# A hybrid decoder layer on one core: output projection's weight tiles split once for two token groups, gate tiles kept in SBUF, fetches one ahead

## The chip, the core and the metric

The kernel runs on one core of a Trainium2 chip. The metric is the device time of one execution in microseconds; the time before is the median of three runs.

## What is computed

One layer of a decoder for 1024 prompt tokens and 8 sequences of 8 new tokens (1088 tokens, width 1024, float32). The reference, cut to what matters here:

```python
h = _rmsnorm(x, g_mix_in)
gate_a, x_a, q, k, v, z_c, xbc, dt_raw = _split_cols(h @ w_in)
...
out_a = h_a * jax.nn.gelu(gate_a)
...
mix = jnp.concatenate([out_a, out_b, out_c], axis=-1) @ w_out
x = x + _rmsnorm(mix, g_mix_out)

hf = _rmsnorm(x, g_ffn_in)
g_f, u_f = jnp.split(hf @ w_gate_up, 2, axis=-1)
x = x + _rmsnorm((jax.nn.silu(g_f) * u_f) @ w_down, g_ffn_out)
```

`out_a` is a gated linear recurrence, `out_b` dilated attention, `out_c` a state space mixer.

## The kernel before

Tokens lie along the free axis, in three groups of 364, 362 and 362 (`GROUPS`); features lie on partitions, in eight chunks of 128. Every product is exact to float32 by three passes: each operand is split into a rounded high part and the rest (`round`, a cast on ScalarE or VectorE; `rest`, a subtraction on VectorE), and TensorE multiplies high by high, low by high and high by low (`mm3`, `x3`). A weight tile of 128x1024 (512 KB) is fetched into one of two raw buffers (`raws`), and split into a pair (`pair`).

The order of the work is set on the host by a planner, the class `Flow`: tasks are Python generators that yield until a condition holds; each operation is costed and handed in with a rank (`RANKS`: "prep" before "mix" before "main"), and the planner writes one fixed instruction list for each engine. VectorE, ScalarE, GpSimd and SyncE (the DMA queue) take the ready operation of the best rank; TensorE's matmuls are emitted as their generators come to them. What a row of the profile calls L345 is the line of the planner that emits all operations but matmuls (L431) and transposes (L435).

The stages around the change:

- `setup` and `first_products`: six warming matmuls on zeros, x loaded and scaled, the first two weight tiles of the input projection multiplied as x arrives.
- The input projection takes weight tiles 0 to 22 in turn. Each tile and group ends in a PSUM bank that `spill` multiplies by the inverse norm on VectorE and, for most tiles, writes to DRAM (`pd`). The last two, `GATE_T` and the next, are the gate.
- `gate`: six pieces (two tiles j, three groups g). A piece is loaded from `pd` with the recurrence's state `hd` into one of three sets of buffers (`shared`), goes through gelu (a square and a tanh on ScalarE, four steps on VectorE), and is split into `XH` and `XL`, the split mixer outputs that the output projection reads. The three sets are free for this when the state space mixer is done (`c_done`).
- `first_out`: the output projection of group 0. Tile n is multiplied over seven of eight chunks while the attention still runs, and copied to SBUF; the eighth chunk comes behind attention's last unit, from one tile of its own (`LATE_T`).
- `second_half`: groups 1 and 2, `out_tile` for n from 0 to 7 each. The weight tiles come from a stream of items (`make_stream`, `streamed`), eight for group 1 and the same eight again for group 2; an item's fetch and split are handed in together (`plain`) as a pair comes free.
- `out_norm(g)`, of rank "prep": first inverse norm (`inverse_norm`: a sum over partitions by matmul, a power on GpSimd, a transpose, a broadcast by matmul), product and residual sum for eight chunks, second inverse norm, scaling into `Y`.
- `right_factors(i)`: for token half i (two quarters of 272 tokens) the factors of a Strassen-like scheme of seven products: parts of `Y` are split, subtracted and split again, each on 128x1088 elements. Factors 1 and 2 need group 0 and 1, 7 and 3 of the first half need group 2; 6, 4, 5 come by subtractions in place.
- `plain_gate_up`, then `gate_up` and `down` on these factors, with weight tiles from the same stream, to the end.

## Time and profile before

| | us |
|---|---|
| median of three runs (1339.01 to 1341.4) | 1340.19 |
| the profiled execution | 1338.55 |
| its span, first to last instruction | 1336.8 |
| mean granted TensorE clock (share of full) | 0.991 |

Times in the rows below are from the start of the span. PE is TensorE's matmuls, PEld its weight loads, DVE VectorE, ACT ScalarE, POOL GpSimd, SP SyncE, which issues the DMAs. A float32 matmul of the program (one of the few that are not split) makes several records. "Idle before" is the time that an engine had nothing to do ahead of a group, with what ended it. Names are the program's without their numbers: t is an SBUF tile, bank a PSUM bank.

### The profile page before, as it was taken

Reading aid. Unit: us, or ns where it says so; the run is one execution under the profiler, and the core shown is the slowest. Engines: PE = TensorE matmul, PEld = TensorE weight load, DVE = VectorE, ACT = ScalarE, POOL = GpSimd, SP = SyncE. Lnnn points to the kernel's source line nnn. Section 1 sums busy time; section 2 is a strip of 40 time slices with the busy share of each in tenths; the row PEclk is TensorE's granted clock in tenths of the full one; section 3 lists DMA queues with packets and bytes.
Section 4 is the critical chain, followed back from the end, with each engine's and each line's share of the span. In section 5 each row is a group of like instructions: output and inputs, shape, how many; then the busy total and the mean of one; then the engine's idle time right before and its main releaser. Section 6 shows DMA issues by size and latency. Waiting matters only on the chain.

```text
span 1336.8 us, 22870 instructions
## 1 busy us (share of the span) xinstructions
PE 1300.9 (97%) x8871; PEld 1243.3 (93%) x8871; DVE 933.1 (70%) x1878; ACT 585.3 (44%) x1095; POOL 19.9 (1%) x36
## 2 busy tenths in 40 slices
PE   9999999999998989989899999999999999999997
PEld 8999988999997878989899999999999999999786
DVE  7799884776858887888766666666567855555852
ACT  7355451752856675544322222222223444444422
POOL 0000000000000000000000000000000000000000
PEclk9999999999999899999999999999999999999999
DMA  6122466456547437635122113221222477865661
GB/s 212 29 68 72 133 184 207 137 175 189 160 130 231 141 103 236 193 116 182 40 97 97 48 51 97 97 80 44 72 97 97 158 237 221 293 210 183 204 205 48
DMA packets 95946, 186.33 MB, mean 139 GB/s; under 512 B 15346, under 2 KB 62686, under 8 KB 95838
## 3 DMA queue, kind: packets, MB, share of 16 engines
q1 hardware_dynamic: 95838, 184.88, 43.9%
q8 instruction: 69, 1.13, 0.3%
q14 instruction: 39, 0.32, 0.1%
HBM read 144.45 MB, written 40.40 MB: 138 GB/s over the span
## 4 chain that ended last, share of the span: by engine, by line
PE 86%; DMA 5%; DVE 3%; issue 2%; ACT 2%; SPq 1%; DVEq 0%; POOLq 0%; POOL 0%; ACTq 0%
PE bank L431 84%; DVE t L345 3%; PE bank L435 2%; DMA t<-pd 2%; ACT t L345 2%; DMA t<-in_w_out_t 2%; DMA t<-in_w_in_t 1%; SPq L345 1%; DMA t<-in_w_gu_t 1%; DMA t<-in_xT 0%; DVEq L2007 0%; POOLq L2007 0%; POOL t L345 0%; DVEq L345 0%; ACTq L345 0%
## 5 line engine op out<-in xcount | busy, mean ns | idle before, releaser
L431 PE MATMUL bank<-t,t 128*128 128x272 f32 (+8 forms) x8505 | 1274.5, 313 | 27.1 <-DVE t L345 13.8
L431 PEld LDWEIGHTS bank<-t,t 128*128 128x128 f32 (+2 forms) x8505 | 1205.0, 187 | 78.6 <-DVE t L345 23.0
L345 DVE TENSOR_TENSOR t<-t,t 128x512 fp32r<-128x512 f32 (+13 forms) x633 | 458.8, 749 | 128.7 <-ACT t L345 112.5
L345 ACT CAST t<-t 128x512 fp32r<-128x512 f32 (+6 forms) x346 | 251.2, 748 | 404.7 <-PE bank L431 159.2
L345 DVE TENSOR_TENSOR t<-t,bank 128x272 f32<-128x272 f32 (+4 forms) x283 | 126.9, 453 | 123.8 <-PE bank L431 122.4
L345 DVE TENSOR_TENSOR t<-bank,t 128x362 f32<-128x362 f32 (+11 forms) x227 | 112.1, 511 | 73.3 <-ACT t L345 43.4
L345 ACT ACTIVATE t<-t,t 128x128 f32<-128x128 f32 (+17 forms) x212 | 132.8, 666 | 34.1 <-DVE t L345 14.7
L345 ACT ACTIVATE t<-t 128x272 f32<-128x272 f32 (+10 forms) x173 | 91.1, 537 | 95.0 <-DVE t L345 90.8
L345 ACT COPY t<-bank 128x272 f32<-128x272 f32 (+8 forms) x122 | 44.5, 372 | 101.3 <-PE bank L431 89.0
L345 DVE TENSOR_TENSOR t<-t 128x272 f32<-128x272 f32 (+8 forms) x147 | 67.5, 459 | 2.8 <-ACT t L345 0.2
L345 DVE SCALAR_TENSOR_TENSOR t<-t,t,t 128x1112 f32<-128x1112 f32 (+7 forms) x68 | 56.6, 860 | 4.7 <-ACT t L345 4.0
L435 PE MATMUL bank<-t,t 128*128 128x128 f32 (+5 forms) x354 | 54.7, 276 | 1.5 <-ACT t L345 0.8
L345 ACT ACTIVATE t<-bank 128x272 f32<-128x272 f32 (+7 forms) x55 | 23.3, 428 | 65.2 <-PE bank L431 63.1
L345 DVE CAST t<-t 128x512 fp32r<-128x512 f32 (+6 forms) x68 | 30.4, 449 | 26.7 <-PE bank L431 13.5
L345 ACT CAST t<-bank 128x512 fp32r<-128x512 f32 (+2 forms) x72 | 35.0, 514 | 31.4 <-PE bank L435 30.5
L435 PEld LDWEIGHTS bank<-t,t 128*128 128x128 f32 (+5 forms) x354 | 40.7, 139 | 7.4 <-DVE t L345 2.4
L345 DVE CUSTOM_DVE_ANT_0 t<-bank,t 128x512 f32<-128x512 f32 (+3 forms) x75 | 39.9, 548 | 7.3 <-PE bank L431 6.7
L345 POOL TENSOR_TENSOR t<-t,t 128x3 f32<-128x3 f32 (+1 forms) x17 | 17.0, 1000 | 1148.2 <-DVE t L345 1082.9
L345 DVE SCALAR_TENSOR_TENSOR t<-t,t,bank 128x362 f32<-128x362 f32 (+4 forms) x55 | 28.2, 550 | 1.6 <-PE bank L431 1.4
L345 DVE SCALAR_TENSOR_TENSOR t<-t 128x54 f32<-128x54 f32 (+5 forms) x39 | 17.9, 458 | 2.5 <-DMA t<-yd 1.6
L345 ACT ACTIVATE t<-bank,t 128x362 f32<-128x362 f32 (+1 forms) x29 | 15.7, 560 | 8.9 <-PE bank L431 8.8
L345 DVE SCALAR_TENSOR_TENSOR t<-t,t 128x1024 f32<-128x1024 f32 (+2 forms) x20 | 17.5, 889 | 1.5 <-ACT t L345 1.4
(20 smaller groups left out, 72.6 us busy)
## 6 DMA issues: line engine op xcount, KB each, us to landing
t<-in_w_dn SPq DMA_DIRECT2D x66, 512.0 KB, 3.7
t<-in_w_gu_t SPq DMA_DIRECT2D x52, 512.0 KB, 4.6
t<-in_w_out_t SPq DMA_DIRECT2D x24, 512.0 KB, 4.2
hidd<-t SPq DMA_DIRECT2D x44, 272.0 KB, 2.1
t<-in_w_in_t SPq DMA_DIRECT2D x21, 512.0 KB, 4.9
t<-hidd SPq DMA_DIRECT2D x44, 176.0 KB, 3.8
t<-pd SPq DMA_DIRECT2D x24, 256.0 KB, 4.1
pd<-t SPq DMA_DIRECT2D x28, 181.0 KB, 3.2
```

Source lines behind the costliest of these rows:

```text
L345: self.flow.note(self.name, what, args, kw, lambda: getattr(self.engine, what)(*args, **kw))
L431: self.flow.product(out, [w, x], start, d, lambda: self.nc.tensor.matmul(out, w, x, **how))
L435: self.flow.product(out, [x], True, d, lambda: self.nc.tensor.transpose(out, x, ident))
```

## The change

- Seven splits of weight tiles instead of sixteen in the second half of the output projection: in `second_half`, tile 7 is used from the pair in which `first_out` left it, and tiles 0 to 6 are split once and serve groups 1 and 2. Their places are a spare pair, five pairs of factor buffers (`IN_TURN`, lent until the factors are formed) and the pair of the late chunk. Group 2 takes them in the order 7, 0, 6, 1 to 5. The first half's factors 7 and 3 now wait until all of group 2's tiles are read (`out_read`).
- `fetch` is split from `plain`: the next item's tile is fetched one ahead, into the other raw buffer.
- The gate's tiles are evicted from PSUM straight into SBUF (`gate_at`) instead of to DRAM and back, and three tasks, one for each group, start as soon as their group's eviction is handed in. Tiles of the gate wait for `c_done` before that; `first_out` waits for all six pieces.
- A rank "norm" between "prep" and "mix" for `out_norm` and the first factors; the factors' subtractions and later splits go to "mix", behind the beginning of the second step of the plain gate-up (`plain_begun`).
- Residual sums are called through another name of the same VectorE queue; eight warming matmuls instead of six, and four more among the first products; the planner costs a matmul anew; outputs of the plain gate-up lie in two new buffers, which become raw buffers when it is done.

In all TensorE has 8254 instructions instead of 8253, VectorE 1760 instead of 1743, ScalarE 863 instead of 896 and SyncE 531 instead of 551.

```diff
-WARM = 6
+WARM = 4
...
+FIRST, IN_TURN = 5, (7, 3, 6, 4, 5)
...
-    RANKS = {"prep": 0, "mix": 1, "main": 2}
+    RANKS = {"prep": 0, "norm": 1, "mix": 2, "main": 3}
...
-            d = max(math.prod(out.shape[1:]), 120) * (1 if x.dtype == F32R else 4) / 2400 + 0.0025
+            n = math.prod(out.shape[1:])
+            d = max(n / 2400 + 0.0135, 0.109) if x.dtype == F32R else max(n, 128) / 600 + 0.0025
...
+            if i >= GATE_T:
+                nc.vector.tensor_mul(self.gate_at(i - GATE_T, g), b, self.rs[:, sl])
+                return
...
+                        if i >= GATE_T:
+                            yield lambda: self.c_done
...
-            nc.vector.memset(squares[0][:, 0:256], 0.0)
-            for _ in range(WARM):
-                self.mm(self.bank[7][:, 0:128], squares[0][:, 0:128], squares[0][:, 128:256], start=True, stop=True)
+            self.zeros = self.alloc(256)
+            nc.vector.memset(self.zeros, 0.0)
+            self.warm(2 * WARM)
...
+                    if k == i == g == 0:
+                        self.warm(WARM)
...
-        F.spawn(self.gate(), group="b")
+        temps = Rot([self.mg[:, 6 + n] for n in range(3)])
+        for g in range(3):
+            F.spawn(self.gate(g, temps), group="b")
...
-        self.splits = [self.pair()] + self.splits
+        self.spare = self.pair()
+        self.open("first")
+        parts = {FIRST: self.factor()}
+        self.open("halves0")
+        parts.update({p: self.factor() for p in IN_TURN[:-1]})
+        self.lent = [[x.rearrange("p k t -> p (k t)")[:, :1024] for x in parts[p]] for p in IN_TURN]
         self.mixers_done = True
         yield lambda: 0 in self.x1_done and not F.pending([self.mg_words])
         self.release(self.mg_pool)
-        self.open("first")
-        first = self.alloc(4, QT, dt=F32R), self.alloc(4, QT, dt=F32R)
-        self.open("halves0")
-        self.XT = [self.half_parts(0, first)]
+        self.open("rest")
+        parts.update({p: self.factor() for p in PRODUCTS if p not in parts})
+        F.spawn(self.right_factors(0, parts), cls="prep")
+        self.XT = [parts]
...
-    def gate(self):
+    def gate_at(self, j, g):
+        return self.mg[:, 3 * j + g, :GROUPS[g][1]]
+
+    def gate(self, g, temps):
         nc, F = self.nc, self.flow
+        c0, w = GROUPS[g]
+        sl = slice(c0, c0 + w)
         for j in range(2):
-            yield lambda: self.emitted > GATE_T + j and self.c_done
-            for g, (c0, w) in enumerate(GROUPS):
-                sl = slice(c0, c0 + w)
-                x, p, h = [t[:, :w] for t in self.shared()]
-                nc.sync.dma_start(x, self.pd[GATE_T + j][:, sl])
-                nc.sync.dma_start(h, self.hd[j][:, sl])
-                nc.scalar.activation(p, x, AF.Square)
-                nc.vector.tensor_scalar(p, p, 0.044715, 1.0, op0=ALU.mult, op1=ALU.add)
-                nc.vector.tensor_mul(p, p, x)
-                nc.scalar.activation(p, p, AF.Tanh, scale=math.sqrt(2.0 / math.pi))
-                nc.vector.scalar_tensor_tensor(x, p, 1.0, x, op0=ALU.add, op1=ALU.mult)
-                nc.vector.scalar_tensor_tensor(h, x, 0.5, h, op0=ALU.mult, op1=ALU.mult)
-                yield lambda: self.free_at[g] == W_OUT_T
-                self.round(self.XH[:, j, sl], h)
-                self.rest(self.XL[:, j, sl], h, self.XH[:, j, sl])
-                self.in_done.add((j, g))
+            yield lambda: self.free_at[g] > GATE_T + j
+            x, p, h = self.gate_at(j, g), temps()[:, :w], self.ev()[:, :w]
+            nc.sync.dma_start(h, self.hd[j][:, sl])
+            nc.scalar.activation(p, x, AF.Square)
+            nc.vector.tensor_scalar(p, p, 0.044715, 1.0, op0=ALU.mult, op1=ALU.add)
+            nc.vector.tensor_mul(p, p, x)
+            nc.scalar.activation(p, p, AF.Tanh, scale=math.sqrt(2.0 / math.pi))
+            nc.vector.scalar_tensor_tensor(x, p, 1.0, x, op0=ALU.add, op1=ALU.mult)
+            nc.vector.scalar_tensor_tensor(x, x, 0.5, h, op0=ALU.mult, op1=ALU.mult)
+        for j in range(2):
+            x = self.gate_at(j, g)
+            self.round(self.XH[:, j, sl], x)
+            self.rest(self.XL[:, j, sl], x, self.XH[:, j, sl])
+            self.in_done.add((j, g))
...
-            self.flow.spawn(self.out_norm(g), cls="prep")
+            self.flow.spawn(self.out_norm(g), cls="norm")
...
+            yield lambda: all((j, g) in self.in_done for j in range(2) for g in range(3))
...
-                self.streamed(0, len(self.splits) - 1)
+                self.streamed(0)
...
-        for _ in range(2):
-            self.items += [lambda pair, t=W_OUT_T + n: self.plain(pair, t) for n in range(KT)]
+        self.items += [lambda pair, t=W_OUT_T + n: self.plain(pair, t) for n in range(KT - 1)]
...
-        self.slots, self.sent, self.hids = {}, 0, {}
-
-    def streamed(self, i, held=0):
-
-        last = min(i + len(self.splits) - 1 - held, len(self.items) - 1)
+        self.slots, self.sent, self.hids, self.places = {}, 0, {}, {}
+        order = [LATE_T] + [W_OUT_T + n for n in range(KT - 1)]
+        order += [W_GU_T + which * NF + f for f in range(PLAIN) for which in range(2)]
+        self.tiles_of = dict(enumerate(order))
+        self.tiles_of.update({self.dn_base + n: W_DN_T + n % NF for n in range(1, 3 * NF)})
+        self.fetched = []
+
+    def streamed(self, i, held=0, alone=False):
+
+        ahead = 0 if i < self.plain_base or alone else len(self.splits) - 1 - held
+        last = min(i + ahead, len(self.items) - 1)
         for j in range(self.sent, last + 1):
             with self.prio("prep"):
-                pair = self.splits.pop(0)
-                self.splits.append(pair)
+                if j in self.places:
+                    pair = self.places[j]
+                else:
+                    pair = self.splits.pop(0)
+                    self.splits.append(pair)
                 self.items[j](pair)
+                if self.tiles_of.get(j + 1) is not None and not self.fetched:
+                    self.fetch(self.tiles_of[j + 1])
             self.slots[j] = pair
         self.sent = max(self.sent, last + 1)
         return self.slots[i]
...
+        self.nc.sync.dma_start(raw.rearrange("p (n c) -> p n c", c=128) if t == LATE_T else raw, src)
+        self.fetched.append((t, raw))
+
+    def plain(self, pair, t):
+        if not self.fetched:
+            self.fetch(t)
+        u, raw = self.fetched.pop(0)
+        assert u == t
+        hi, lo = [x[:, :raw.shape[-1]] for x in pair]
         self.round(hi, raw)
         self.rest(lo, raw, hi)
...
-        i = 1
-        for g in (1, 2):
-            for n in range(KT):
-                yield from self.out_tile(g, n, self.streamed(i))
-                i += 1
+        last, late = self.splits
+        self.splits = [last, self.spare, late]
+        slots = [self.spare] + self.lent + [late]
+        self.places = dict(enumerate(slots, 1))
+        held = [(KT - 1, last)] + list(enumerate(slots))
+        for at, (n, pair) in enumerate(held):
+            self.streamed(min(at + 2, KT - 1))
+            yield from self.out_tile(1, n, pair, at)
+        for at, (n, pair) in enumerate(held[:2] + held[-1:] + held[2:-1]):
+            yield from self.out_tile(2, n, pair, at)
+            self.out_read = at + 1
+            if at < len(self.splits):
+                self.streamed(KT + at, alone=True)
...
-        self.XT.append(self.half_parts(1))
-        self.raws.items += [self.alloc(1024) for _ in range(2)]
-        self.raws.i = 1
+        self.XT.append({p: self.factor() for p in PRODUCTS})
+        F.spawn(self.right_factors(1, self.XT[1]), cls="prep")
+        self.late_raws = [self.alloc(1024) for _ in range(2)]
...
-        def split(p, x):
+        first = "mix" if i else "norm"
+
+        def split(p, x, cls="mix"):
             hi, lo = parts[p]
-            self.round(hi, x)
-            self.rest(lo, x, hi)
-
-        split(1, b11)
-        split(2, b21)
+            with self.prio(cls):
+                self.round(hi, x)
+                self.rest(lo, x, hi)
+
+        def sub(out, x, y):
+            with self.prio("mix"):
+                nc.vector.tensor_sub(out, x, y)
+
+        split(1, b11, first)
+        split(2, b21, first)
         self.quarters = max(self.quarters, 1)
-        yield lambda: i + 1 in self.x1_done
+        yield lambda: i + 1 in self.x1_done and (i or self.out_read == KT)
         if i == 0:
-            split(7, b12)
-        split(3, b22)
+            split(7, b12, first)
+        split(3, b22, first)
         self.quarters = 2
-        self.nc.vector.tensor_sub(b11, b12, b11)
-        self.nc.vector.tensor_sub(b12, b22, b12)
-        self.nc.vector.tensor_sub(b22, b22, b11)
+        yield lambda: i or self.plain_begun
+        sub(b11, b12, b11)
+        sub(b12, b22, b12)
+        sub(b22, b22, b11)
         split(6, b22)
-        self.nc.vector.tensor_sub(b21, b21, b22)
+        sub(b21, b21, b22)
         split(4, b21)
         split(5, b11)
...
+            out = outs()
...
+                self.plain_begun = f > 0
...
         self.plain_done = True
+        self.raws = Rot(self.raws.items + self.late_raws)
+        self.raws.i = 1
```

The order in which instructions stand, at two places. The first is VectorE around the last evictions of the input projection (t2 is `XL`, t17 the eviction buffers, t110 before and t111 after the buffers of the gate, bank0 and bank6 the projection's banks). Before, the second gate tile's group 0: its last two gelu steps and its rest (the last row), which stands 64 VectorE instructions behind its eviction:

```order
L345 TENSOR_TENSOR t2_74<-t110_2152,t1_73 128x362
L345 TENSOR_TENSOR t136_2181<-bank7_69,t136_2181 64x256
L345 ISA t122_2167,t141_2186<-bank1_63,t146_2191 128x128
L345 ISA t141_2186 128x1
L345 SCALAR_TENSOR_TENSOR t110_2152<-t110_2152 128x364
L345 TENSOR_SCALAR t110_2152<-t110_2152 128x362
L345 SCALAR_TENSOR_TENSOR t110_2152<-t110_2152 128x364
L345 TENSOR_TENSOR t110_2152<-t110_2152 128x362
L345 TENSOR_SCALAR t110_2152<-t110_2152 128x362
L345 TENSOR_TENSOR t2_74<-t110_2152,t1_73 128x364
```

Now the same piece: the step ahead of these rows is its first one, and the rest is again the last row, 20 instructions behind its eviction:

```order
L347 TENSOR_TENSOR t2_74<-t111_2132,t1_73 128x364
L347 TENSOR_TENSOR t111_2132<-bank6_68,t16_99 128x362
L347 TENSOR_TENSOR t111_2132<-t111_2132 128x364
L347 TENSOR_TENSOR t2_74<-t17_100,t1_73 128x364 x3
L347 SCALAR_TENSOR_TENSOR t111_2132<-t111_2132 128x364
L347 TENSOR_TENSOR t134_2158<-bank3_65,t133_2157 128x512
L347 SCALAR_TENSOR_TENSOR t111_2132<-t111_2132,t17_100 128x364
L347 TENSOR_TENSOR t136_2160<-bank4_66,t135_2159 128x384
L347 TENSOR_TENSOR t111_2132<-bank0_62,t16_99 128x362
L347 ISA t127_2151,t145_2169<-bank2_64,t147_2171 128x512
L347 ISA t145_2169 128x1
L347 TENSOR_TENSOR t2_74<-t111_2132,t1_73 128x364
```

The piece's whole chain now stands between the evictions of the second tile's other groups (the two rows that read bank6 and bank0 and t16); before it stood behind all of them, and behind attention's rows.

The second place is VectorE at the third group's norm, ahead of the first half's factors (t156 before and t157 after are `Y` and the groups' sums; outputs of 128x1088 with an fp32r source pair are rests of factors; t7 is the spread norm). Before, rests and subtractions in place stand ahead of the third group's first residual product (last row):

```order
L345 TENSOR_TENSOR t172_5240<-t156_4872,t171_5239 128x1088
L345 TENSOR_TENSOR t156_4872<-t156_4872 128x4x272
L345 TENSOR_TENSOR t168_5236<-t156_4872,t167_5235 128x1088
L345 TENSOR_TENSOR t156_4872<-t156_4872 128x4x272
L345 TENSOR_TENSOR t7_82<-bank3_65,t3_78 6x256
L345 TENSOR_TENSOR t156_4872<-t156_4872 128x4x272
L345 TENSOR_TENSOR t162_5230<-t156_4872,t161_5229 128x1088
L345 TENSOR_SCALAR t7_82<-bank3_65,t3_78 6x106
L345 TENSOR_TENSOR t158_4874<-t188_5539,t157_4873 128x1024
L345 TENSOR_TENSOR t170_5238<-t156_4872,t169_5237 128x1088
L345 TENSOR_TENSOR t156_4872<-t156_4872,bank6_68 128x272
L345 TENSOR_TENSOR t156_4872<-t156_4872,bank3_65 128x362
```

Now the second group's scaling, then two rests, then the third group's norm and its first residual product and sum:

```order
L347 SCALAR_TENSOR_TENSOR t157_4851<-t157_4851,t4_79,bank1_63 128x362 x8
L347 TENSOR_TENSOR t16_99<-t16_99,t17_100 128x362
L347 TENSOR_TENSOR t163_4863<-t157_4851,t162_4862 128x1088
L347 TENSOR_TENSOR t165_4865<-t157_4851,t164_4864 128x1088
L347 TENSOR_SCALAR t8_83<-bank3_65 128x3
L347 CAST t8_83<-t8_83 128x3
L347 TENSOR_TENSOR t8_83<-t8_83 128x3
L347 TENSOR_TENSOR t7_82<-bank3_65,t3_78 6x256
L347 TENSOR_SCALAR t7_82<-bank3_65,t3_78 6x106
L347 TENSOR_TENSOR t157_4851<-t157_4851,bank3_65 128x362
L347 TENSOR_TENSOR t188_5527<-t188_5527,bank6_68 128x272
L347 TENSOR_TENSOR t157_4851<-t157_4851,t17_100 128x362
```

The subtractions and three of the rests have moved behind the third group's residual.

## Rows read from the trace of the kernel before

**Rows 1.** The page, busy time by engine: us, share of the span, instructions.

```profile
PE 1300.9 (97%) x8871; PEld 1243.3 (93%) x8871; DVE 933.1 (70%) x1878; ACT 585.3 (44%) x1095; POOL 19.9 (1%) x36
```
**Rows 2.** Stretches (from:to, length): busy by engine, then PEclk, DMA share, GB/s.

```profile
421.60:437.10 15.50, 8.58 (x58) 6.55 (x57) 13.74 (x40) 13.32 (x32) 0.00 (x0) 0.97 0.64 190
437.10:501.60 64.50, 59.05 (x376) 54.37 (x377) 52.58 (x118) 44.60 (x96) 0.00 (x0) 0.93 0.40 121
501.60:511.40 9.80, 7.82 (x35) 6.58 (x36) 6.84 (x16) 3.32 (x6) 0.85 (x1) 0.83 0.70 224
511.40:564.00 52.60, 52.58 (x320) 51.23 (x320) 44.19 (x80) 29.49 (x49) 2.05 (x2) 1.00 0.68 211
564.00:590.00 26.00, 21.50 (x134) 19.79 (x133) 20.62 (x35) 10.27 (x15) 2.62 (x2) 0.93 0.49 162
590.00:645.00 55.00, 50.80 (x383) 49.71 (x382) 49.90 (x77) 28.07 (x41) 1.87 (x1) 0.97 0.40 129
645.00:1336.80 691.80, 683.99 (x4812) 665.50 (x4811) 426.94 (x764) 229.09 (x409) 4.27 (x5) 1.00 0.40 129
```
**Rows 3.** Timeline of PE, 420 to 646 us: start, length, group, [idle before, releaser].

```profile
437.14 9.11 PE L431 MATMUL bank<-t,t 128*128 128x364 f32 x36 [2.27 <-ACT t L345]
...
507.79 0.85 PE L431 MATMUL bank<-t,t 128*128 128x362 f32 x2 [1.50 <-ACT t L345]
...
583.72 0.39 PE L431 MATMUL bank<-t,t 128*128 128x272 f32 x1 [1.61 <-ACT t L345]
...
585.79 14.41 PE L431 MATMUL bank<-t,t 128*128 128x272 f32 x96 [1.68 <-DVE t L345]
...
638.45 0.39 PE L431 MATMUL bank<-t,t 128*128 128x272 f32 x1 [2.11 <-ACT t L345]
...
640.93 5.30 PE L431 MATMUL bank<-t,t 128*128 128x272 f32 x28 [2.09 <-DVE t L345]
```
**Rows 4.** Stretches in which the granted clock was 0.50, columns as in rows 2.

```profile
436.27:443.10 6.83, 5.96 (x19) 5.68 (x20) 5.19 (x10) 3.72 (x11) 0.00 (x0) 0.50 0.51 160
494.30:497.71 3.41, 3.41 (x15) 3.07 (x14) 3.28 (x7) 2.77 (x6) 0.00 (x0) 0.50 0.00 0
...
sum 20.47, PE 19.11 PEld 17.86 DVE 18.61 ACT 9.88 POOL 0.00; mean PE 3.82 PEld 3.57 DVE 3.72 ACT 1.98 POOL 0.00
```
**Rows 5.** Timeline of SP (DMA issues), 421 to 434 us.

```profile
431.42 1.17 SPq L345 DMA_DIRECT2D t<-pd  x2
```
**Rows 6.** Three stretches with VectorE nearly full, columns as in rows 2.

```profile
371.00:487.00 116.00, 107.56 (x732) 99.61 (x730) 85.93 (x223) 74.47 (x161) 0.00 (x0) 0.97 0.57 167
...
584.00:600.00 16.00, 14.32 (x97) 13.73 (x97) 16.00 (x20) 8.46 (x10) 0.00 (x0) 0.89 0.08 20
...
620.00:641.00 21.00, 16.80 (x129) 16.20 (x129) 20.27 (x26) 12.67 (x17) 0.00 (x0) 1.00 0.20 65
```
**Rows 7.** Instructions by line and shape, VectorE and ScalarE: busy us, mean ns, idle before.

```profile
L345 DVE TENSOR_TENSOR t<-t,t 128x1024 fp32r<-128x1024 f32 x125 | 152.6, 1223 | 78.6 <-ACT t L345 77.7
...
L345 DVE TENSOR_TENSOR t<-t,t 128x1088 fp32r<-128x1088 f32 x17 | 21.6, 1282 | 1.2 <-ACT t L345 1.2
...
L345 ACT CAST t<-t 128x1024 fp32r<-128x1024 f32 x111 | 116.3, 1048 | 148.8 <-DMA t<-in_w_dn 81.0 <-PE bank L431 19.1 <-DMA t<-in_w_in_t 17.5
```
**Rows 8.** The page's DMA issues: count, KB each, median us to landing.

```profile
t<-in_w_out_t SPq DMA_DIRECT2D x24, 512.0 KB, 4.2
```
**Rows 9.** Timeline of VectorE, 569 to 600 us.

```profile
570.47 0.16 DVE L345 TENSOR_SCALAR t<-bank 128x3 f32<-128x3 f32 x1 [0.48 <-PE bank L431]
...
572.71 0.77 DVE L345 CAST t<-t 128x1024 fp32r<-128x1024 f32 x2 [0.49 <-DMA t<-in_w_gu_t]
...
580.37 0.58 DVE L345 SCALAR_TENSOR_TENSOR t<-t,t,bank 128x362 f32<-128x362 f32 x1
```
**Rows 10.** Timeline of PE, 0 to 14 us.

```profile
1.22 2.93 PE L431 MATMUL bank<-t 128*128 128x128 f32 x12 [1.22 <-DVE t L345]
...
7.22 7.03 PE L431 MATMUL bank<-t,t 128*128 128x362 f32 x24 [1.23 <-ACT t L345]
```

60 lines of the change are left out of this document (30 added, 30 removed).

## The prediction

> **What bounds the kernel now.** I read the page first, for the shares [rows 1]. TensorE is busy for 1300.9 of 1336.8 us and its weight loads for 1243.3, so nothing that other engines gain is worth anything unless TensorE waits for it. All that a change of order can win is TensorE's 35.9 us without work, and what its clock loses after them. The next view is the table of stretches [rows 2]: from 645 us to the end (gate-up products and down projection, 691.8 us) TensorE has work for 683.99 us at full clock, so the change has little to win there. The idle time lies in four short places between 421 and 645 us. The third view, TensorE's timeline, names each wait and who ends it [rows 3]: ScalarE or VectorE each time, never another matmul. The fourth is the granted clock [rows 4]: five stretches at 0.50 (1.2 of 2.4 GHz) stand behind such waits (the group shows the longest, one of the other four, which are 3.41 us each, and the sum), with 19.11 us of TensorE work in them, which at full clock would have taken 9.6 us less. A wait therefore costs its length and about 1.7 us (half of 3.41) behind it, 3.0 us behind the longest.
>
> So the stock from which the change can draw, stretch by stretch (idle from rows 2, clock as half of the busy time in rows 4), is:
> - A, 421.6 to 437.1 (gate): 6.9 idle and 3.0 clock, 9.9 us
> - B, 437.1 to 501.6 (end of attention): 5.5 and 1.7, 7.2 us
> - C, 501.6 to 511.4 (second group's first tiles): 2.0 and 1.5, 3.5 us
> - D, 564 to 590 (norms, factors 7 and 3): 4.5 and 1.7, 6.2 us
> - E, 590 to 645 (first product): 4.2 and 1.7, 5.9 us
>
> Together 32.7 us.
>
> **The gate (A and B).** Before, a gate tile's group goes to DRAM and comes back: SyncE issues the loads for the second gate tile only at 431.42 us [rows 5], when one of three sets of temporaries has come free. Behind that stand a square and a tanh on ScalarE, four steps on VectorE and the split, and TensorE waits until 437.14 [rows 3]. The change takes out six writes and six reads, and lets each group's chain start at its own eviction. The order shows the whole chain of the second tile's first group standing within the evictions, so its rest is due 20 VectorE rows behind its eviction instead of 64. First products of the output projection now also wait for all six gate pieces, and the attention units run on meanwhile. Nothing is added on VectorE: an eviction, four steps and a rest for each piece, as before.
>
> But this is a stretch in which VectorE is nearly full: 13.74 of 15.5 us there [rows 2], 85.93 of 116.00 from 371 to 487 us [rows 6]. What no longer makes TensorE wait there is done elsewhere in the same 130 us, and seven weight splits of the second half are pulled up to its end as well. From both sides: nothing (the waits only move within A and B), or all 17.1 us. A's waits, the one at 437.14 with the clock behind it (2.3 and 3.0) above all, belong to the gate's chain and should go but for a rest of one; B's belong to attention's own chains of maxima and sums, which the change leaves as they are. So I take most of A and nothing of B: **−9.0**.
>
> **Second half of the output projection (C).** Before, sixteen tiles of 512 KB are fetched and split, eight for each group; now the last tile of the first group is used again and seven are split once. Gone are nine fetches (4.2 us from issue to landing each [rows 8], beside other work), nine casts (ScalarE 1.05) and nine rests (VectorE 1.22 [rows 7]): 9.4 us and 11.0 us of engines that are not the bound there; at 511.4 to 564 TensorE is busy 52.58 of 52.60 us [rows 2]. So the nine splits by themselves are worth **0**, hidden under the group's 192 matmuls; if that cover were gone they would cost 20. What pays is their time. The second group's first tile waits for nothing now: its pair is the one just used, and the next was fetched ahead. Before, TensorE waited 1.50 us at 507.79 for a pair whose raw tile had just landed, and ran at half clock behind that. From nothing to all 3.5; I take **−3.0**, since the norm of the first group still ends there.
>
> **Norms and factors (D).** Before, VectorE forms the second group's sums at 570.47 and reaches the scaling only at 580.37 [rows 9], 9.9 us for a chain of eight short steps, because weight splits stand between, one of them waiting for its tile. Factors 7 and 3 need this, and TensorE waits 1.61 and 1.68 us for them at 583.72 and 585.79 [rows 3]. In the change no split stands there, and the norms have a rank ahead of the splits and of the factors' subtractions. VectorE's next rows are the two rests of 1.28 us [rows 7] instead of five with four subtractions between. The gap between the two waits closes, and so does the clock's loss. The lower end is nothing (VectorE is full from 584 to 600, 16.00 of 16.00 us [rows 6]: what is put first displaces something), the upper 6.2. I take **−4.5**, as the norm's own chain (a power on GpSimd, a transpose, a broadcast) stays.
>
> **First product (E).** The waits at 638.45 and 640.93 (2.11 and 2.09) are for factor 6 of the second half of the tokens, behind VectorE's 20.27 busy of 21.00 us [rows 3, 6]. The third group's residual started late, since nine operations of 1088 elements stood ahead of it; with the order changed it starts some 11 us earlier (those nine by 1.28). TensorE's place for factor 6 is the same. So a wait of 4.2 us should be covered, against a new load of at most nine operations that come in between. From nothing to 5.9; I take **−4.4**. Late there next is that factor's own subtraction, which needs the third group's x1.
>
> **The start.** TensorE's six warming products end at 4.15 us; its second run of products comes in at 7.22 after a wait of 1.23, and takes 7.03 us for 24 matmuls [rows 10], 0.293 each against 0.164 later. Two warming products more ahead of it and four in between can bring the clock up earlier, worth 3.1 us if nothing else held the matmuls; but x arrives and is scaled no sooner. At the other end the six took 2.93, so two more cost 0.98 and four 1.95, of which the wait covers 1.23: +1.7. Between these I take **−0.5**, near nothing, since the wait shows the operands behind.
>
> **Edits at nothing.** "Residual sums on VectorE" swaps one name for the planner's for the same engine: no instruction changes engine. The planner's new matmul cost has no instruction of its own; it is in the order that I read. The plain gate-up's outputs in raw buffers that come later: gate-up streams 0.5 MB tiles under TensorE's 684 us.
>
> **Sum**: −9.0 −3.0 −4.5 −4.4 −0.5 = −21.4. The profiled execution took 1338.55 us, so 1317.15; the median of the runs is 1340.19, 1.64 above that execution, so **1318.8**.
>
> **Rivals.**
> 1. VectorE sets the pace of A and B, and the waits move. For it: its 13.74 of 15.5 us; its work up to the first group's norm rises by some 7 us of splits. Against it: 30 us of 116 are idle there. Then only C, D, E and the start come: −12.4, 1327.8. Chance 0.17.
> 2. VectorE's queue holds back what is behind it. The row at 570.47 and the 9.9 us after it [rows 9] show a scaling of half a microsecond waiting behind splits that themselves wait for a transfer. Seven splits now stand in one bunch in front of the first group's norm; should a fetch be late there, norms and factors all shift, and D and E keep their waits: −12.5, 1327.7. Against: the second and third group's products, over 60 us of TensorE, lie between. Chance 0.14. The Trainium skill has the rule, in "TensorE: Matmul & The Clock Gate", section "Architectural detail": ScalarE and VectorE take their instructions strictly in order, and only TensorE pulls weight loads ahead. By that rule the bunch holds the norm for as long as its slowest fetch; the trace agrees at 570.47, and shows no instruction of VectorE passing another.
> 3. All of it goes: 32.7 and the start's 0.5, 1307.0. For: every wait named has a cause that the change touches or moves. Against: attention's chains in B are as they were. Chance 0.10.
> 4. Slower: one tile ahead is too little. The seven tiles, if they go one by one, take 4.2 to land, 1.05 to be cast and 1.22 for the rest, 6.5 us each, against 24 matmuls of 0.164 (52.58 by 320 [rows 2]), 3.9 us. Seven times 2.5 is 17.7, and each wait leaves 1.7 at half clock, 11.9 in all; with only A, B's 9.0 and the start's 0.5 left as gains that is +20.1, 1360.3. It decides against the change from 5.3 us a tile on (21.4 by 7 is 3.1, of which 1.7 clock). Against: two raw buffers in turn make it 3.2 us a tile, and the planner issues the fetches while the first group still runs. Chance 0.08.
> 5. The order's gain is nil, since waits come up elsewhere by as much: 1340. Chance 0.05.
>
> **How the numbers follow.** A difference under 0.2% (2.7 us) cannot be told from none. The forecast has 0.46, with a range of its own from 1312 to 1326 (A and B between −4 and −14). Faster: 0.46 + 0.17 + 0.14 + 0.10 = 0.87; same 0.05; slower 0.08. The range leaves out rivals 4 and 5 and half of rival 3: 1309 to 1331, the upper end rivals 1 and 2 with 3 us for their unknowns.
>
> **What would show it.** A and B: no wait over 1 us for XH or XL between 420 and 440, and the granted clock at 1.00 there; if VectorE's busy share to the first norm is over 90% with TensorE waiting for it, it is rival 1. C: the second group's first tile follows the first group's last without a wait for a weight; waits of 2 us or more at a constant distance of some 6 us would be rival 4. D: the second group's scaling within 5 us of its sums. E: no wait of 2 us within the first product. The prediction is wrong if TensorE's busy time leaves 1300 by over 10 us (then the loss was clock, or matmuls), or if the stretch behind 645 us changes by over 5 us.

## The result and the profile after

The changed kernel takes 1325.51 us (median of four runs, 1324.68 to 1328.14), the kernel before 1340.03 beside it: a ratio of 0.9899, 95% interval 0.9881 to 0.9917, or 14.5 us less by the medians. It is 1% faster and lies inside the ranges of the prediction, at the upper edge of the narrower one (1312 to 1326). The forecast of 1318.8 was too low by 6.7 us: two thirds of the 21.4 us came. Rivals 1 and 2, at 1327.8 and 1327.7, are nearer in number; the stretches below show that what they describe is not what happened.

The page of the kernel after, its span and its busy times (before [rows 1]):

```profile
span 1324.1 us, 22869 instructions
...
PE 1295.8 (98%) x8883; PEld 1238.6 (94%) x8883; DVE 935.5 (71%) x1890; ACT 558.6 (42%) x1064; POOL 18.0 (1%) x36
```

TensorE's idle time fell from 35.9 us to 28.3 (1324.1 less 1295.8), and its mean granted clock rose from 0.991 to 0.995. To add both up, I use one measure from here on, **lost time**: the part of a stretch in which TensorE had no work, plus half of its busy time at half clock (worked out from the trace in steps of a tenth of a microsecond). It is 45.5 us before and 33.3 after. The 12.2 us between them are nearly all of the 12.7 by which the span fell, so the matmuls were done with less waiting. In the variants below the change of lost time and that of the span agree within 3.2 us, and within 4.6 in the one with the gate alone. Stretches of the kernel before, columns as in [rows 2]:

```profile
0.00:40.00 40.00, 36.51 (x193) 34.82 (x193) 28.04 (x53) 26.73 (x49) 1.46 (x8) 1.00 0.51 178
40.00:400.00 360.00, 358.58 (x2443) 334.55 (x2442) 273.59 (x648) 188.26 (x377) 6.79 (x17) 1.00 0.46 137
400.00:500.00 100.00, 87.66 (x553) 79.94 (x552) 81.92 (x211) 69.64 (x149) 0.00 (x0) 0.95 0.55 160
500.00:520.00 20.00, 17.87 (x99) 16.34 (x99) 14.22 (x30) 9.18 (x15) 0.85 (x1) 0.91 0.70 225
...
560.00:645.00 85.00, 76.30 (x539) 73.50 (x538) 74.53 (x119) 40.26 (x60) 4.49 (x3) 0.96 0.45 145
```

The same stretches of the kernel after:

```profile
0.00:40.00 40.00, 37.96 (x219) 36.51 (x220) 29.16 (x57) 26.95 (x49) 2.33 (x9) 1.00 0.51 178
40.00:400.00 360.00, 352.09 (x2392) 326.20 (x2391) 270.81 (x639) 186.86 (x376) 5.95 (x16) 1.00 0.46 133
400.00:500.00 100.00, 94.98 (x623) 88.17 (x622) 83.76 (x216) 71.47 (x148) 0.00 (x0) 0.98 0.55 158
500.00:520.00 20.00, 17.68 (x90) 16.89 (x89) 12.26 (x21) 8.12 (x14) 1.77 (x1) 0.83 0.56 174
...
560.00:645.00 85.00, 82.01 (x619) 79.64 (x618) 75.14 (x124) 39.20 (x62) 2.90 (x3) 1.00 0.35 111
```

The first number behind the comma is TensorE's busy time. From 400 to 500 us it was 87.66 of 100 and is 94.98; from 560 to 645 it was 76.30 of 85 and is 82.01. Against that, from 40 to 400 us it was 358.58 of 360 and is 352.09: a stretch of which the prediction did not speak now waits 7.9 us. By stretch, in lost time:

| us | what stands there | forecast | before | after | difference |
|---|---|---|---|---|---|
| 0 to 40 | start | −0.5 | 3.5 | 2.0 | −1.5 |
| 40 to 400 | input projection and mixers | 0 | 1.4 | 7.9 | **+6.5** |
| 400 to 500 | gate, end of attention (A, B) | −9.0 | 17.0 | 6.7 | −10.3 |
| 500 to 520 | first group's norm, second group's first tiles (C) | −3.0 | 3.6 | 5.6 | **+2.0** |
| 560 to 645 | norms, factors, first product (D, E) | −8.9 | 12.1 | 3.0 | −9.1 |
| 645 to end | products, down | 0 | 7.8 | 8.0 | +0.2 |

TensorE's timeline after, the longest waits (before [rows 3]):

```profile
156.83 4.73 PE L434 MATMUL bank<-t,t 128*64 128x128 f32 x40 [1.16 <-DVE t L347]
...
186.50 3.74 PE L434 MATMUL bank<-t,t 128*64 128x192 f32 x27 [1.31 <-DMA t<-in_ssd_state]
...
333.28 1.09 PE L438 MATMUL bank<-t,t 128*128 128x128 f32 x8 [1.21 <-DMA t<-pd]
...
413.93 0.41 PE L434 MATMUL bank<-t,t 128*128 128x384 f32 x1 [1.78 <-ACT t L347]
...
507.93 7.84 PE L434 MATMUL bank<-t,t 128*128 128x1 f32 x30 [2.32 <-DVE t L347]
...
595.73 6.25 PE L434 MATMUL bank<-t,t 128*128 128x1 f32 x48 [0.83 <-DVE t L347]
...
628.16 4.79 PE L434 MATMUL bank<-t,t 128*128 128x272 f32 x36 [1.18 <-DVE t L347]
```

Of the six waits in [rows 3] none is left at its place at that length: 437.14 (2.27), 507.79 (1.50, for a weight's split) and the pairs before factors 7 and 6 are gone. D's stretch (564 to 590) has no wait left, and E's keeps 0.83 at 595.73, 1.18 at 628.16 and a shorter one. New are three waits of 1.2 to 1.3 us in the mixers, two of them for transfers; the other 4.2 us there are waits of 0.75 us or less, most of them for VectorE. New are also two waits in front of and behind the gate's old place: 413.93, for a cast that waits for a projection read back (ScalarE):

```profile
411.48 1.99 ACT L347 CAST t<-t 128x1024 fp32r<-128x1024 f32 x2 [4.99 <-DMA t<-pd]
```

and 507.93, for sums of the first group's norm. That last one is worth following back. SyncE, then ScalarE, then VectorE:

```profile
485.95 0.45 SPq L347 DMA_DIRECT2D mixd<-t  x1
487.87 0.33 SPq L347 DMA_DIRECT2D t<-mixd  x1
496.43 0.45 SPq L347 DMA_DIRECT2D mixd<-t  x1
496.99 2.08 SPq L347 DMA_DIRECT2D t<-in_w_out_t  x2
```

```profile
500.85 1.05 ACT L347 CAST t<-t 128x1024 fp32r<-128x1024 f32 x1 [2.09 <-DMA t<-in_w_out_t]
```

```profile
496.44 0.69 DVE L347 CAST t<-t 128x1024 fp32r<-128x1024 f32 x1
497.05 2.69 DVE L347 TENSOR_TENSOR t<-t,t 128x364 f32<-128x364 f32 x4
501.93 1.22 DVE L347 TENSOR_TENSOR t<-t,t 128x1024 fp32r<-128x1024 f32 x1 [2.19 <-ACT t L347]
503.86 0.69 DVE L347 CAST t<-t 128x1024 fp32r<-128x1024 f32 x1 [0.71 <-DMA t<-in_w_out_t]
504.86 3.01 DVE L347 TENSOR_TENSOR t<-t,t 128x362 fp32r<-128x362 f32 x5 [0.30 <-ACT t L347]
```

From 487.87 to 496.43 SyncE's queue stands still behind a write of attention's last piece (`mixd`). The fetch of a weight tile, whose raw buffer the late chunk's split had left at 483.5, stands behind that write and goes out at 496.99. ScalarE casts it at 500.85, VectorE's rest at 501.93 has waited 2.19 us for that, the next split at 503.86 another 0.71 for its own fetch, and the last sums of group 0 stand behind both in VectorE's queue: the row at 504.86 holds them, up to 507.87. TensorE waits until 507.93, 2.32 us, and runs at half clock to 514.4, which loses 3.2 more. The Trainium skill ("TensorE: Matmul & The Clock Gate", "Architectural detail") has VectorE and ScalarE strictly in order; these rows agree, with 2.19 and 0.71 us.

D went as its step said: the second group's scaling now starts 4.4 us behind its sums (9.9 in [rows 9]), with only the norm's own chain and two additions of 0.54 us between:

```profile
562.31 0.15 DVE L347 TENSOR_SCALAR t<-bank 128x3 f32<-128x3 f32 x1
...
566.74 4.11 DVE L347 SCALAR_TENSOR_TENSOR t<-t,t,bank 128x362 f32<-128x362 f32 x8 [0.31 <-PE bank L434]
```

### The profile page after: what moved, and what is told of

Same layout as the page of the kernel before. It is cut to its first block, busy times and chain, and to the rows that moved or that the text cites. A ratio compares the mean times of both kernels' runs of the same rounds, so it can differ in the third digit from the quotient of the medians.

```text
span 1324.1 us, 22869 instructions
## 1 busy us (share of the span) xinstructions
PE 1295.8 (98%) x8883; PEld 1238.6 (94%) x8883; DVE 935.5 (71%) x1890; ACT 558.6 (42%) x1064; POOL 18.0 (1%) x36
## 4 chain that ended last, share of the span: by engine, by line
PE 76%; DVE 9%; DMA 9%; ACT 2%; issue 2%; SPq 1%; DVEq 0%; POOLq 0%; POOL 0%; ACTq 0%
PE bank L434 74%; DVE t L347 9%; ACT t L347 2%; DMA t<-pd 2%; DMA t<-in_w_in_t 2%; PE bank L438 2%; SPq L347 1%; DMA t<-mixd 1%; DMA t<-in_w_out_t 1%; DMA t<-acd 1%; DMA t<-eacd 1%; DMA t<-in_ssd_state 0%; DMA t<-yd 0%; DMA t<-in_w_gu_t 0%; DMA t<-hidd 0%
## 5 line engine op out<-in xcount | busy, mean ns | idle before, releaser
L434 PE MATMUL bank<-t,t 128*128 128x272 f32 (+6 forms) x8505 | 1266.4, 312 | 16.6 <-DVE t L347 11.8
L434 PEld LDWEIGHTS bank<-t,t 128*128 128x128 f32 (+1 forms) x8505 | 1199.5, 186 | 65.3 <-DVE t L347 22.0
L347 ACT CAST t<-t 128x512 fp32r<-128x512 f32 (+7 forms) x315 | 221.8, 726 | 442.6 <-PE bank L434 188.7
L347 DVE TENSOR_TENSOR t<-bank,t 128x512 fp32r<-128x512 f32 (+11 forms) x227 | 111.7, 511 | 76.0 <-ACT t L347 42.0
L347 ACT ACTIVATE t<-t 128x272 f32<-128x272 f32 (+9 forms) x173 | 91.5, 537 | 114.0 <-DVE t L347 108.2
L347 DVE CAST t<-t 128x1024 fp32r<-128x1024 f32 (+6 forms) x90 | 44.4, 494 | 46.9 <-PE bank L434 34.8
L347 ACT COPY t<-bank 128x272 f32<-128x272 f32 (+7 forms) x122 | 44.5, 373 | 78.1 <-PE bank L434 64.8
L347 DVE SCALAR_TENSOR_TENSOR t<-t,t,t 128x1112 f32<-128x1112 f32 (+6 forms) x68 | 56.8, 860 | 5.1 <-ACT t L347 4.3
L347 DVE CUSTOM_DVE_ANT_0 t<-bank,t 128x512 f32<-128x512 f32 (+4 forms) x75 | 39.8, 548 | 5.2 <-PE bank L434 4.8
L347 DVE SCALAR_TENSOR_TENSOR t<-t,t 128x1024 f32<-128x1024 f32 (+4 forms) x26 | 20.3, 804 | 3.9 <-DMA t<-hd 2.4
```

The costliest lines, as they stand in the source:

```text
L347: self.flow.note(self.name, what, args, kw, lambda: getattr(self.engine, what)(*args, **kw))
L434: self.flow.product(out, [w, x], start, d, lambda: self.nc.tensor.matmul(out, w, x, **how))
```

## The experiments

All times are ratios to the kernel before on the same chip, with their intervals. Twelve variants ran. Lost time by stretch, in us, from one profile of each (the start and what stands behind 645 us are left out):

| kernel | ratio (95%) | 40–400 | 400–500 | 500–520 | 520–560 | 560–645 |
|---|---|---|---|---|---|---|
| before | 1 | 1.4 | 17.0 | 3.6 | 0.0 | 12.1 |
| after | 0.9899 (0.9881–0.9917) | 7.9 | 6.7 | 5.6 | 0.0 | 3.0 |
| before, new matmul cost | 1.0057 (1.0034–1.0080) | 6.1 | 16.5 | 3.6 | 0.8 | 13.0 |
| before, gate | 1.0058 (1.0034–1.0082) | 1.3 | 19.6 | 10.2 | 0.0 | 15.2 |
| before, gate and cost | 1.0041 (1.0025–1.0058) | 6.1 | 7.4 | 6.5 | 0.0 | 21.5 |
| after without gate | 0.9963 (0.9943–0.9983) | 9.1 | 12.1 | 2.1 | 1.7 | 2.4 |
| after without ranks | 0.9931 (0.9911–0.9951) | 7.2 | 8.9 | 3.6 | 0.0 | 6.8 |
| after, one split less ahead | 0.9892 (0.9865–0.9920) | 9.4 | 7.2 | 0.9 | 0.9 | 3.0 |
| after, fetch two ahead | 0.9892 (0.9855–0.9930) | 9.0 | 8.1 | 0.9 | 0.0 | 3.5 |
| after, floor by width | 0.9905 (0.9873–0.9936) | 9.2 | 8.2 | 5.5 | 0.0 | 2.3 |
| after, margin | 0.9935 (0.9914–0.9955) | 10.4 | 12.6 | 1.3 | 0.0 | 4.8 |
| after, margin and one split less | 0.9928 (0.9901–0.9954) | 8.2 | 9.5 | 0.0 | 0.0 | 5.1 |
| after, slower transfers in the plan | **0.9805** (0.9788–0.9822) | 3.0 | 2.9 | 0.0 | 3.9 | 3.6 |
| before, slower transfers in the plan | 1.0116 (1.0079–1.0152) | 1.7 | 17.6 | 5.7 | 1.7 | 11.5 |

The changed kernel and the one with one split less have the same order up to 500 us, and lose 7.9 and 9.4 us from 40 to 400: differences of up to some 1.5 us between two kernels are not to be read in these columns.

**The planner's matmul cost alone, on the kernel before.**

```diff
-            d = max(math.prod(out.shape[1:]), 120) * (1 if x.dtype == F32R else 4) / 2400 + 0.0025
+            n = math.prod(out.shape[1:])
+            d = max(n / 2400 + 0.0135, 0.109) if x.dtype == F32R else max(n, 128) / 600 + 0.0025
```

> The kernel before, with one edit: the planner costs a matmul as in the changed kernel. Lost time is span minus TensorE's busy time at its granted clock. Theory: the new waits of the changed kernel in the mixers (lost time from 40 to 400 us 7.9 us, before 1.4) come from the order that this cost gives. Then here 5 to 9 us are lost between 40 and 400 us, and the time is about 1344. Rival: they come from the other edits; then 1 to 2 us as before, and 1340 within 3.

1347.04 us, slower by 0.57%, with 6.1 us lost from 40 to 400:

```profile
40.00:400.00 360.00, 353.86 (x2403) 328.54 (x2404) 272.00 (x643) 186.75 (x375) 6.80 (x17) 1.00 0.46 133
400.00:500.00 100.00, 87.80 (x560) 80.50 (x559) 75.97 (x198) 64.28 (x137) 0.00 (x0) 0.93 0.56 166
```

The theory holds for the mixers: an edit that emits no instruction makes them wait. The likely way is that the planner takes matmuls to be longer than before and so holds an operand to be ready behind fewer of them; the run shows the waits, not this step. The time is 3 us above the expected 1344; behind 645 us, where nothing was expected, 2.5 us more are lost.

**The gate alone, on the kernel before.** The new `gate`, `gate_at`, the branch in `spill`, and the two conditions (`c_done`, all six pieces).

> The kernel before with the gate's part alone: gate tiles evicted into SBUF, one task for each group, first products of the output projection behind all six pieces. Theory: the gate's part makes the gain from 400 to 500 us (lost time there 17.0 before, 6.8 in the changed kernel): 7 within 2 here, about 1330. Rival: the end of attention gains by the planner's new cost or the second half's stream and not by the gate; then about 12 are lost, 1335.

1346.07 us, slower by 0.58%: both theory and rival missed. The loss moved to later places and grew:

```profile
400.00:500.00 100.00, 88.67 (x551) 82.00 (x550) 83.91 (x219) 70.48 (x149) 0.85 (x1) 0.89 0.49 147
500.00:520.00 20.00, 14.40 (x61) 13.31 (x62) 12.72 (x26) 5.92 (x11) 1.07 (x1) 0.69 0.67 211
```

At its own place the gate's part does what it was meant for. From 420 to 440 us TensorE's idle time falls from 7.0 us to 2.9, nearly all of it one wait of 2.74 at 426.59, and with the clock the loss from 420 to 480 falls by 6.2, to 5.1. From 480 to 520 it rises from 9.2 to 23.4. There the first group's norm, earlier now and of rank "prep", comes ahead of attention's last unit on VectorE: from 495.75 on, products and sums of 364 elements (residuals of the first group) stand in front of the attention's eviction at 502.44,

```profile
495.75 1.42 DVE L345 TENSOR_TENSOR t<-t,bank 128x364 f32<-128x364 f32 x3 [1.51 <-PE bank L431]
497.08 1.43 DVE L345 TENSOR_TENSOR t<-t,t 128x364 f32<-128x364 f32 x3
...
500.21 1.41 DVE L345 TENSOR_TENSOR t<-t,bank 128x364 f32<-128x364 f32 x3
...
502.44 0.68 DVE L345 TENSOR_TENSOR t<-bank,t 128x512 fp32r<-128x512 f32 x1
```

for which TensorE waits 5.35 us:

```profile
503.18 1.11 PE L431 MATMUL bank<-t,t 128*128 128x256 f32 x4 [5.35 <-DVE t L345]
```

**The changed kernel without the gate's part**, its counterpart (old `gate` and `spill`, conditions out).

> The changed kernel with the gate as before (through DRAM, one task, three sets of buffers). The gate alone on the kernel before gained nothing. Theory: with the rest of the change in place the gate's part does bring the gain from 400 to 500 us (6.7 us lost in the changed kernel, 17.0 before): 13 to 19 are lost there, 1334 or more. Rival: that gain is the planner's cost and the second half's; 6 to 10 are lost, 1326 within 2.

1334.29 us, 0.9963, as the theory had it; 12.1 us lost from 400 to 500, between the two expectations. In this company the gate's part is worth 5.4 us there, and some 0.6% in all (0.9963 against 0.9899). The other 4.9 us of that stretch (17.0 to 12.1) come without it.

**Gate and matmul cost, on the kernel before.** Both edits above.

> The kernel before with the gate's part and the planner's new matmul cost, nothing else. With the gate alone 19.6 us were lost from 400 to 500 us and 10.2 from 500 to 520, since the first group's norm came ahead of attention's last steps on VectorE. Theory: with the new cost the planner keeps them apart, and the gate's gain comes: under 10 lost from 400 to 500, 3 to 6 from 500 to 520; with the mixers' 5 us more and the factors' waits as before, 1335 within 3. Rival: the gain needs fewer splits or the rank of the norms: 17 or more from 400 to 500, 1345 or more.

From 400 to 500 us the theory holds: 7.4 us lost, where each edit alone left 16.5 or more. The total does not follow, 1344.76, 1.0041, since the norms and factors lose 21.5 us:

```profile
400.00:500.00 100.00, 94.28 (x612) 86.40 (x610) 81.98 (x212) 71.97 (x149) 0.00 (x0) 0.98 0.55 152
...
560.00:645.00 85.00, 70.04 (x476) 67.38 (x475) 71.49 (x115) 38.80 (x56) 6.79 (x3) 0.88 0.44 144
```

Neither edit makes a gain from 400 to 500 us alone, the pair makes the 10 us, and then needs the rest of the change so as not to lose them 100 us later.

**Ranks as before, in the changed kernel.** Norms, splits and subtractions back at "prep", no `plain_begun`.

```diff
-            self.flow.spawn(self.out_norm(g), cls="norm")
+            self.flow.spawn(self.out_norm(g), cls="prep")
...
-        first = "mix" if i else "norm"
+        first = "prep"
...
-        yield lambda: i or self.plain_begun
```

> The changed kernel with norms, factors and subtractions at their old rank, and no wait for the second step of the plain gate-up. Theory: the order of norms ahead of factors' work makes the gain between 560 and 645 us (lost there 12.1 before, 2.9 in the changed kernel): then 9 to 13 come back, about 1334. Rival: nine splits less on VectorE are enough; then at most 5 are lost there, 1326 within 2.

1329.78 us; 6.8 us lost from 560 to 645, between theory and rival. Of the 9.1 us that D and E gained, 3.8 hang on the ranks and the wait for `plain_begun`, and 5.3 stay without them. That these are the nine splits less is likely and not shown, as no run puts the splits back. In the total the two kernels are barely apart (0.9931 against 0.9899, their intervals touch).

**One split less ahead.**

```diff
-            self.streamed(min(at + 2, KT - 1))
+            self.streamed(min(at + 1, KT - 1))
```

> The changed kernel, in which a tile of the second half is split one tile ahead of its use instead of two. Theory: TensorE's wait of 2.32 us at 507.93 and the 6.8 us at half clock behind it come from sums of the first group's norm that stand on VectorE behind splits waiting for their fetches. With one split less in front the wait goes: lost time from 500 to 520 us falls from 5.5 to under 1.5, about 1321. Rival: the sums are late by attention's last steps themselves, or the missing split makes TensorE wait for weights: 5 us or more stay lost, 1325 or above.

**Fetches two ahead.** The next fetch but one is handed in as well while tiles of the output projection are left.

```diff
-                if self.tiles_of.get(j + 1) is not None and not self.fetched:
-                    self.fetch(self.tiles_of[j + 1])
+                ahead = 2 if j + 2 < self.plain_base else 1
+                while len(self.fetched) < ahead and self.tiles_of.get(j + 1 + len(self.fetched)) is not None:
+                    self.fetch(self.tiles_of[j + 1 + len(self.fetched)])
```

> The changed kernel with weight tiles of the second half fetched two ahead, so that one fetch is issued before attention's last write on the SyncE queue instead of behind it; one split more then stands on VectorE ahead of the first group's sums. Theory: order on VectorE decides, every split in front that waits for its fetch delays the sums: 4 us or more are lost from 500 to 520 (5.5 in the changed kernel, 0.9 with one split less), 1325 within 2. Rival: the late issue behind attention's write is the cause; under 1.5 lost, 1321.

1324.16 and 1324.36 us. In both the loss from 500 to 520 us falls from 5.6 to 0.9, but not in the same way. I measure from the end of attention's last eviction on VectorE to the last sum of group 0: 11.5 us in the changed kernel (496.40 to 507.87), 8.6 with one split less (499.33 to 507.96), 13.4 with two fetches ahead (500.01 to 513.42). With one split less the sums come 2.9 us sooner by this measure, as the theory has it, and the wait shrinks to 0.92 us although the norm's matmul stands 9 matmuls earlier:

```profile
508.01 3.98 PE L434 MATMUL bank<-t,t 128*128 128x1 f32 x24 [0.92 <-DVE t L347]
```

With two ahead they come later, as that theory has it too, since two splits in front wait for their fetches (VectorE):

```profile
505.84 0.69 DVE L347 CAST t<-t 128x1024 fp32r<-128x1024 f32 x1 [1.50 <-DMA t<-in_w_out_t]
...
508.47 0.69 DVE L347 CAST t<-t 128x1024 fp32r<-128x1024 f32 x1 [0.68 <-DMA t<-in_w_out_t]
...
512.89 2.11 DVE L347 TENSOR_TENSOR t<-t,t 128x364 f32<-128x364 f32 x3
```

and yet TensorE waits only 0.84 us:

```profile
513.47 2.90 PE L434 MATMUL bank<-t,t 128*128 128x1 f32 x18 [0.84 <-DVE t L347]
```

for the planner now puts the norm's matmul 21 matmuls later, some 3.4 us by 0.164. So the expectation's number fell with its mechanism standing, and the rival's number came for a reason of neither. Nor does this run take the late issue away: the fetch for which the split at 505.84 waits goes out at 502.34, again behind attention's last write (500.04). Whether the issue behind that write is the cause stays open. In the total neither gain can be seen: 0.9892 each, against 0.9899 with intervals of 0.002 to 0.004. The 4.7 us of that stretch are shown by the profile, not by the times.

**The least matmul cost by width of the weights.**

```diff
-            d = max(n / 2400 + 0.0135, 0.109) if x.dtype == F32R else max(n, 128) / 600 + 0.0025
+            d = max(n / 2400 + 0.0135, 0.109 * m / 128) if x.dtype == F32R else max(n, 128) / 600 + 0.0025
```

> The changed kernel, in which the least cost of a matmul goes with the width of its weights (0.109 us for 128 columns, half for 64) instead of 0.109 for all; 64-column weights with 128 columns of data are spaced 57 to 68 ns in the trace. Theory: the mixers' new waits (7.9 us lost from 40 to 400 us) come from narrow matmuls that the planner takes to be too long: under 4 us lost there, about 1321. Rival: they come from the higher cost of wide matmuls; 6.5 or more, 1325.

9.2 us lost from 40 to 400, 1326.22 us: the theory falls, the narrow matmuls' floor is not what makes the mixers wait. That the cost of the wide ones does, as the rival has it, is left over and not tested by itself.

**A larger margin, and the margin with one split less.** `MARGIN` 1.0 for 0.2.

> The changed kernel, in which a generator takes an operand as ready 1.15 us after the planner's end of it instead of 0.35 (MARGIN 1.0 for 0.2). The new matmul cost brought 4.7 us of waits into the mixers although it is nearer to the measured spacing of wide matmuls. Theory: the old, too short matmul cost was a hidden reserve: it left the planner's own matmuls behind their operands; without it operands of attention and mixers are late by 1 to 2 us. A margin gives that back: lost from 40 to 400 us at most 4 (7.9 in the changed kernel), the wait at 413.93 gone, about 1320. Rival: the waits are from orders on SyncE and VectorE that a margin does not move; 7 or more stay, 1325.

> The margin of 1.15 us together with a split one tile ahead of its use instead of two. Theory: the two gains add: under 4 lost from 40 to 400 us and under 1.5 from 500 to 520, about 1317. Rival: the margin alone shifts the first group's norm as well, or lets TensorE wait for weights in the second half: 1322 or above.

1330.83 and 1328.13 us, neither faster than the changed kernel: the first is some 0.4% slower (0.9935 against 0.9899, intervals just touching), the second (0.9928) can't be told from it. The wait at 413.93 goes, but 10.4 and 8.2 us are lost from 40 to 400 and 12.6 and 9.5 from 400 to 500, with a new wait of 4.10 and 4.33 us for VectorE around 435. A general reserve for all operands moves the waits; it doesn't stand for what the short matmul cost had given. The theory of a hidden reserve of that kind falls, and so does the one that the two gains add.

**Slower transfers in the plan.**

```diff
-    QUEUE, FLIGHT, RECEIPT, RATE = 0.475, 0.65, 0.95, 360e3
+    QUEUE, FLIGHT, RECEIPT, RATE = 0.475, 0.65, 1.95, 250e3
```

> The changed kernel, in which the planner takes transfers to be slower (receipt 1.95 for 0.95 us, 250 for 360 GB/s). Theory: late transfers (states, projections read back, weight tiles) are what the mixers and the gate's stretch wait for; 5 or less lost from 40 to 400 us, and under 4 from 400 to 420, about 1321. Rival: the waits end with VectorE's chains, and the transfers' model matters little or moves other work behind: 7 or more, 1325 or above.

1312.99 us, 0.9805: better than the theory asked for, and the fastest of all. TensorE is busy for 357.04 of 360, 97.08 of 100 and 20.00 of 20 us in the three stretches:

```profile
40.00:400.00 360.00, 357.04 (x2429) 332.03 (x2428) 273.87 (x649) 187.80 (x378) 6.28 (x17) 1.00 0.47 138
400.00:500.00 100.00, 97.08 (x648) 90.27 (x648) 85.67 (x217) 78.20 (x163) 0.85 (x1) 1.00 0.54 160
500.00:520.00 20.00, 20.00 (x125) 20.00 (x124) 15.09 (x29) 10.98 (x20) 0.00 (x0) 1.00 0.68 226
520.00:560.00 40.00, 36.88 (x223) 35.15 (x222) 33.80 (x74) 17.64 (x31) 3.76 (x4) 0.96 0.43 133
```

A new wait stands before the third group's norm, 2.42 us, with the granted clock at 0.50 for 10.24 us from 556.95 on:

```profile
558.49 0.37 PE L438 MATMUL bank<-t,t 128*6 128x128 f32 x1 [2.42 <-DVE t L347]
```

**The same edit on the kernel before**, the control.

> The kernel before with the planner's slower transfers alone (receipt 1.95 for 0.95 us, 250 for 360 GB/s), the control for the same edit on the changed kernel, which took that one from 1325 to 1313. Theory: the edit removes waits behind late transfers that the changed kernel's matmul cost and early gate had uncovered (40 to 420 us, and the first group's norm at 508); the kernel before loses only 1.4 us from 40 to 400 us, so it gains little: 1340 within 4. Rival: the planner's transfers are too short for any order; then it gains about as much, 1328 within 4, and the change's own worth on top stays 15.

1354.41 us, 1.0116: both missed, it is 1.2% slower. Lost time rises by 3.2 us from 645 to 1000 and by 11.2 behind 1000, where before the kernel was nearly full; the largest single wait there, 7.93 us at 1172.63, is for a cast that ScalarE starts after 11.36 us of waiting for its hidden tile:

```profile
1170.32 0.48 ACT L345 CAST t<-t 128x352 fp32r<-128x352 f32 x1 [11.36 <-DMA t<-hidd]
```

So the slower transfers are no better model as such; they suit the changed kernel's order. Which of its waits went because a transfer was placed well, and which by the new order's chance, the runs do not tell.

## Why the prediction was right or wrong

**Where the time lies** was right but for C: the gain came from A, B, D and E, by the waits and the clock behind them. D and E, −8.9, measured −9.1: 3.8 of it hang on the ranks, and 5.3 on what is left, the nine splits as far as is known. That VectorE was full from 584 to 600 did not stop it. E had more room than its step gave it: the third group's residual starts at 576.95 us, 20.4 before the 597.33 of the kernel before, where the step said some 11. One reading in D was wrong: the norms did not get a rank ahead of the weight tiles' splits, which keep "prep", the better rank; "norm" stands ahead of the factors' subtractions and later splits alone.

**A and B**: −9.0, measured −10.3, a number that is partly luck. I took most of A, by the gate's chain, and nothing of B; it came as about half of each. B fell from 7.2 us to 2.3. A fell from 9.9 to 4.5: its waits between 421 and 437 are gone, but one of 1.78 at 413.93 came up ahead of them, with the clock behind it, for a projection that is read back late. The gate alone clears its own place and loses more behind it; only with the new matmul cost does the gain stay, and within the whole change the gate's part is 5.4 of the 10.3. Rival 1 (the waits only move) is what the gate does alone; in the whole change it is held off by the rest.

**C** failed in sign: −3.0, measured +2.0. The step said that the second group's first tile waits for nothing, which is so. It took no account of the norm's sums, which stand behind those tiles' splits on VectorE; with one split less in front they are 2.9 us sooner. Rival 2 named that mechanism and its place, but priced it at D and E, where it did no harm, instead of at the first group's norm: 5.5 us there (2.32 idle and 3.2 clock). How many matmuls the planner puts ahead of the norm's counts as much: with two fetches ahead the sums come later still, and TensorE waits less.

**The edit at nothing** was the largest mistake: "the planner's new matmul cost has no instruction of its own; it is in the order that I read". I read the order at two places where TensorE waited before, and not from 40 to 400 us, where it didn't and where the cost moves instructions of every mixer. It costs 4.7 us there on the kernel before (6.1 less 1.4). In the whole change 6.5 more are lost there; that this is the same cost at work is likely and not shown, since no run puts the old cost into the changed kernel, and with slower transfers in the plan and the new cost in place only 3.0 are lost there in all. By lost time the change came 9.2 us short of the forecast (12.2 for 21.4): 6.5 in the mixers and 5.0 at C, less 2.3 gained beyond the forecast at the start and in the other places.

**The signs named** all came as they should: no wait of 1 us from 420 to 440, no wait for a weight behind the first group's last tile, the second group's scaling 4.4 us behind its sums, no wait of 2 us in the first product, and TensorE's busy time within 10 us of 1300. None of them looks at the mixers, or asks what TensorE waits for at the first group's norm, and there the forecast failed.

**Rival 4** (one tile ahead is too little) did not come: no row of waits for weights at a constant distance of some 6 us, and the fetch issued late cost its wait through VectorE's sums, not through the tile. **The start** gave 1.5 instead of 0.5. The step took it that operands hold the first products back; but where the first run of them in the kernel before was spaced 0.293 us [rows 10], the changed kernel's are spaced 0.168 (149 in 25.05 us from 8.13 on), at a granted clock that both traces show as 1.00. By 30 us it has 133 products behind it instead of 123.

## What to carry to other kernels

In a kernel whose order a planner writes, what an edit is worth depends on the rest of the kernel: gate and cost are each 0.6% slower alone, together they take 10 us out of one stretch (and are still 0.4% slower, until the rest of the change is there), and the same edit of the transfers' model gives 0.95% on one kernel and takes 1.2% on the other. So compare the written order over the whole program, above all in stretches that were full before, and measure the pair as well as the parts. A late operand is found by following queues, not only data: here a weight fetch stood behind an unrelated write on SyncE, and a norm behind that weight's split on VectorE.
